# Attention scores of a two-block network: two fp32r passes over stacked exact parts, and the convolution's norm moved from the attention into the gates

## The chip, the cores and the metric

The kernel runs on one core of a Trainium2 chip. The time is the device time of that core in microseconds; before the change three runs gave 3316.32, 3317.76 and 3319.42 us. The core's engines are TensorE (PE, with its weight loads PEld), VectorE (DVE), ScalarE (ACT), GpSimd (POOL) and SyncE (SP, which here issues DMAs). Each engine runs its own instructions in order.

## The reference, cut to what matters

The first block is a mixture of an mLSTM and a spatial gating unit over 512 tokens of width 2048. The second block is two hybrid layers over 528 tokens (16 meta tokens ahead of the 512). In each layer the input is projected to a gated convolution, an attention with 16 heads of 64 on 4 key/value heads, and a recurrence:

```python
c = c_val * sigmoid(c_glu)
c = causal_depthwise_conv(c, conv_dw_w, conv_dw_b)        # 31 taps, 512 channels
c = silu(layer_norm(c, conv_ln_g, conv_ln_b))
c = c @ conv_pw_w + conv_pw_b
y_conv = c * silu(c_gate)
q, k = partial_rotary(q), partial_rotary(k)
# scores q.k / 8 on: the 128 keys before, the query's own block of 128, 16 meta keys
att = sliding_window_sink_attention(q, k, v, sinks)
y_attn = att * silu(a_gate)
y_lru = rg_lru(conv(r_x)) * silu(r_gate)
h = layer_norm(alpha * h + concat(y_conv, y_attn, y_lru) @ w_out)
```

All of it is float32 and is computed to float32's precision.

## The kernel before, in words

**Products.** A large product a.b is done in three passes of TensorE in the fp32r format (`mm3`, lines 131 to 139): both operands are split into an exact high part (`hi`, a cast on ScalarE) and the rest (`lo`, a subtraction), and hi.hi, hi.lo and lo.hi are added in PSUM. Weights come by DMA in chunks of 512 KB (`weights`, lines 109 to 129): SP loads, ScalarE casts (L125), VectorE subtracts (L128); while `share` is set every other subtraction is GpSimd's. Small products (attention scores, transposes) are plain float32 matmuls, which the trace shows as two records each, a weight load and a matmul twice over.

**Memory.** Most tiles live in one pool of `NSLOT` = 62 slots of 128 x 530 floats (`slot`). A slot is free again when the last reader of its tile is done; who needs one waits. Products of the projections go to two PSUM accumulators (`acc`), small ones to four PSUM banks (`bank`).

**Order.** The kernel is written in one program order; a planner gives every engine its fixed order, ahead of the run, from its own estimate of times: of the instructions that are ready, the one that stands first in the program goes first, and a later one fills a gap. So projections that stand behind the attention in the program run on TensorE between the attention's short matmuls.

**First block's end.** `sgu_all` loops over 8 heads; each has three projections through `acc` (`vps`, `ups`, `zps`). The two tiles `yg` of a head are slots that receive gelu of `ups` (L536) and stay until the block's output product. The normed input holds 32 slots until the last `zps`, the results before hold 16 + 2 a head.

**A layer of the second block** (`layer`, from L860): after the raw projections, for each of two groups g of 8 heads: one projection for keys (`keys`), four for queries (`rotary`), then `attend`. Behind the group 0 come the 8 projections of the convolution (`conv31`: 4 tiles, each a chain of 31 VectorE instructions, L1159 and L1162). Behind group 1 come 16 gate projections (`gate`) with the pointwise product of the convolution (`pointwise`) before the last four. The layer ends with the split of y and the output product (`out2`, `out2_last`).

**Scores.** A tile of q holds two heads, 64 partitions each. Group g's keys are two tiles: `k`, and `kx` with its halves exchanged, each with the 16 meta keys behind every block of 128 keys. `attend_block` (L1047 on) takes four pairs of heads; each head is one float32 matmul with 64 rows (L1064: 128 queries stationary, 272 keys moving, 144 in the first block), the two heads of a pair on the two halves of the array's rows, into a bank each. VectorE adds the mask and takes the maximum (L1067), ScalarE the exponentials, GpSimd and ScalarE scale, TensorE transposes (L1092) and multiplies with the values (L1099).

**The convolution's norm.** `conv_norm` (L1174 on) is a generator in three steps: sums over the channels (GpSimd adds, `halves` on TensorE into two banks), the squares' sums, then the normed tiles and their split. Before, `attend` of group 1 runs one step behind each of its first blocks of queries (`next(others, None)`).

Of the kernel before, what the change touches and what calls it, by code (L numbers as in the profile page):

```python
# [19 lines left out]
P = 128  # L20
# [11 lines left out]
NSLOT = 62  # L32
# [25 lines left out]
def log1p_of_unit(nc, out, e, pool, shape, tag):  # L58
    """out = log(1 + e) for e in [0, 1], by 2*atanh(e / (2 + e))."""
# [13 lines left out]
class Net:  # L73
# [30 lines left out]
    def after(self, ins, other):  # L104
        """Order two instructions for the scheduler (slots of one pool are taken in that order)."""
        self.tc.add_manual_dep(ins.ins, other.ins.name, mybir.DependencyInfo(mybir.DependencyClass.NoSync, mybir.DependencyReason.DATA),
                               reason="slots in order")

    def weights(self, view, more=None):
        """One chunk of weights [P, k, cols] (k * cols <= 1024, with the columns of `more`) as its two exact parts."""  # L110
# [20 lines left out]
    def mm3(self, outs, wh, wl, xh, xl, first, last):  # L131
        """Three passes of (wh + wl)^T (xh + xl) into the regions outs = [(psum, slice of x)]."""
# [8 lines left out]
    def stack(self, name, parts, pool=None, rows=None):  # L141
        """Vectors whose lengths are multiples of 128, as columns of 128 entries on partitions."""
# [18 lines left out]
    def bcast_rows(self, cols, n, ps):  # L161
        """[P, n] per-token columns (token = chunk * 128 + partition) to a row [P, n * 128] on all partitions."""
# [6 lines left out]
    def block1(self):  # L169
        nc, a, tc = self.nc, self.a, self.tc  # L170
        with ExitStack() as ctx:
# [4 lines left out]
            self.cst1 = pool("cst1", 1)  # L176
            self.xT = self.dram.tile([KT, P, S], F32, name="xT")
# [18 lines left out]
    def load_x(self):  # L196
        """x * norm_w with features on partitions, split, and the sums of the tokens' squares."""
# [33 lines left out]
    def norm_x(self):  # L231
        """The same, times the tokens' factors, which are returned as a row."""
# [15 lines left out]
    def proj1(self, col):  # L248
        """Columns [col, col + 256) of x @ w_in, features on partitions: [P, 2 x 512]."""
# [11 lines left out]
    def proj1_tok(self, col, more=None):  # L261
        """The same columns, tokens on partitions: [P, 256] of each chunk, and 16 columns `more` behind them."""
# [10 lines left out]
        for k0, k1 in zip(bounds, bounds[1:]):  # L273
            ks = slice(k0, k1)
            wh, wl = self.weights(w[:, ks], g[:, ks] if g is not None else None)
            for k in range(ks.start, ks.stop):
                for c, o in enumerate(outs):
                    xh, xl = self.Xh[k][:, c * P:(c + 1) * P], self.Xl[k][:, c * P:(c + 1) * P]
                    # the first product of a bank clears it
# [7 lines left out]
    def gates1(self, gs):  # L287
        """From input and forget gates of all heads [token, gate] of each chunk, what the chunks need of them."""
# [53 lines left out]
        # state factors on all partitions: [P, head, chunk]  # L342
# [11 lines left out]
        # 0 where key <= query, else a large negative number: [key, query]  # L354
# [5 lines left out]
    def conv_silu(self, ps, ch, scale, rb=None):  # L360
        """Causal convolution over 4 tokens and silu of one tile of channels (times rb first, where it is given)."""
# [18 lines left out]
    def mlstm_all(self):  # L380
        nc = self.nc
        for pair in range(NH // 2):
# [9 lines left out]
            for j in range(2):  # L392
                h = pair * 2 + j
                vps = self.proj1_tok(2048 + h * 256, 8192 if h == 0 else None)
                # values with a column of ones, split
# [101 lines left out]
    def sgu_all(self):  # L497
        nc, a = self.nc, self.a
        mm = nc.tensor.matmul
        for h in range(NH):  # L500
            ws = self.sm1.tile([P, P], F32, tag="ws", name="ws", bufs=1)
            nc.gpsimd.dma_start(ws, a["w_spatial"][h])
            # keep source <= target; halved, the other half of silu
# [30 lines left out]
            for i in range(2):  # L534
                t = self.slot(S, name="yg")
# [20 lines left out]
    def out1(self):  # L556
        """h = x + y @ w_out; the two norms in one; splits the result for the second block."""
# [12 lines left out]
        for at in range(0, KT, CG):  # L570
# [23 lines left out]
            # before the results' slots are taken, which wait for the products  # L594
# [47 lines left out]
    def raw_split(self, i, z, g, b, t0):  # L642
        """z * g of tile i, split, with g and b as two more tokens."""
# [14 lines left out]
    def normal(self, i, g, b):  # L658
        """Tile i of the layer's input, split."""
# [18 lines left out]
    def from_raw(self, t):  # L678
        """The product with the layer's input, from that with raw [P, 528 tokens, g, b]."""
# [11 lines left out]
    def token_sums(self, sums, chunks):  # L691
        """Sums over partitions of each tile of `sums`, divided by the width: [token, sum, chunk]."""
# [23 lines left out]
    def token_bcast(self, out, col, chunks):  # L716
        """Per-token columns to rows on all partitions, in out[:, chunk]."""
# [142 lines left out]
    def layer(self, l, last):  # L860
# [39 lines left out]
        for i in (0, 1, 2, 3):  # L900
            gate(4 + i, 3072 + i * P)
# [503 lines left out]
```

## Time and profile before

| | before |
|---|---|
| runs | 3316.32, 3317.76 (median), 3319.42 us |
| profiled execution, first to last instruction | 3318.8 us |
| PE busy | 3241.4 us (98%) |
| PEld busy | 2819.8 us |
| DVE busy | 1829.6 us (55%) |
| ACT busy | 1099.5 us (33%) |
| POOL busy | 745.6 us (22%) |
| granted TensorE clock, mean | 0.990 |

The profiled execution is one more execution of the same program; its span is 1.0 us above the runs' median. Busy is the union of an engine's instructions. On PE each record lasts from a matmul's start to its modelled end, and the next one starts before that end, so the distance between starts is what a matmul takes up in a stream.

### The profile page before, as it was taken

What the parts mean: (1) busy time and instruction counts of PE and PEld (TensorE: products, weight loads), DVE (VectorE), ACT (ScalarE), POOL (GpSimd) and SP (SyncE); (2) the same over time, 40 slices, a digit from 0 to 9 for tenths busy, and PEclk for the clock granted to TensorE, in tenths of its full rate; (3) what the DMA queues carried; (4) which work ended last, traced back from release to release, by engine and by line L of the source; (5) the groups of instructions that cost most, each with busy time, mean ns of one, the idle gap of its engine ahead of it and who ended that gap; (6) DMA issues with size and microseconds to landing.
All of it is one profiled execution on the core that took longest, in us unless ns stands there. A gap on an engine that the chain in (4) does not pass through costs nothing. (4 is left out here: it accounts for less than half of the span.)

```text
span 3318.8 us, 46937 instructions
## 1 busy us (share of the span) xinstructions
PE 3241.4 (98%) x19245; PEld 2819.8 (85%) x19245; DVE 1829.6 (55%) x2931; ACT 1099.5 (33%) x1775; POOL 745.6 (22%) x756
## 2 busy tenths in 40 slices
PE   8999999999999999999998999999999999999996
PEld 7888888888888888877778988989999888777885
DVE  8744454534433333556659698352545969634545
ACT  5332323323222222434433533342322353234322
POOL 3000000000100000012355523343244542444302
PEclk9999999999999999999998999999999999999998
DMA  5322222322333333333232222222332222322333
GB/s 185 96 89 89 89 85 88 89 89 84 100 91 93 96 92 94 104 106 104 101 98 68 75 71 64 71 64 84 90 90 77 84 66 64 89 77 70 114 121 108
DMA packets 348280, 299.35 MB, mean 90 GB/s; under 512 B 11312, under 2 KB 313296, under 8 KB 348064
## 3 DMA queue, kind: packets, MB, share of 16 engines
q1 hardware_dynamic: 343008, 287.35, 28.3%
q0 software_dynamic: 5056, 9.00, 1.0%
q8 instruction: 151, 2.47, 0.3%
q14 instruction: 65, 0.53, 0.1%
HBM read 287.91 MB, written 8.39 MB: 89 GB/s over the span
## 5 line engine op out<-in xcount | busy, mean ns | idle before, releaser
L125 ACT CAST whi<-raw 128x1024 fp32r<-128x1024 f32 (+1 forms) x526 | 549.6, 1045 | 1461.9 <-PE acc L137 1076.0
L128 DVE TENSOR_TENSOR wlo<-raw,whi 128x1024 fp32r<-128x1024 f32 (+1 forms) x456 | 582.2, 1277 | 798.4 <-ACT whi L125 790.9
L139 PE MATMUL acc<-Xh,wlo 128*128 128x512 f32 x1280 | 509.1, 398 | 0.0
L135 PE MATMUL acc<-Xh,whi 128*128 128x512 f32 x1280 | 507.7, 397 | 1.4 <-ACT Xh L223 1.4
L137 PE MATMUL acc<-Xl,whi 128*128 128x512 f32 x1280 | 504.9, 394 | 1.7 <-DVE Xl L224 1.7
L139 PE MATMUL acc<-Hh,wlo 128*128 128x264 f32 (+1 forms) x1792 | 447.7, 312 | 1.3 <-POOL wlo L128 1.3
L137 PE MATMUL acc<-Hl,whi 128*128 128x264 f32 (+1 forms) x1792 | 445.8, 311 | 0.0
L135 PE MATMUL acc<-Hh,whi 128*128 128x264 f32 (+1 forms) x1792 | 444.7, 311 | 0.3 <-ACT xr L675 0.3
L139 PEld LDWEIGHTS acc<-Hh,wlo 128*128 128x128 f32 x1792 | 292.4, 189 | 29.1 <-issue 10.2
L137 PEld LDWEIGHTS acc<-Hl,whi 128*128 128x128 f32 x1792 | 291.8, 189 | 27.7 <-issue 10.1
L135 PEld LDWEIGHTS acc<-Hh,whi 128*128 128x128 f32 x1792 | 292.0, 189 | 24.2 <-issue 5.8
L139 PEld LDWEIGHTS acc<-Xh,wlo 128*128 128x128 f32 x1280 | 241.1, 188 | 57.0 <-issue 2.2
L137 PEld LDWEIGHTS acc<-Xl,whi 128*128 128x128 f32 x1280 | 241.0, 188 | 56.5 <-DVE Xl L224 2.2
L135 PEld LDWEIGHTS acc<-Xh,whi 128*128 128x128 f32 x1280 | 241.0, 188 | 53.2 <-ACT Xh L223 1.8
L284 PE MATMUL acc<-whi,Xl 128*128 128x256 f32 x960 | 269.5, 281 | 0.0
L282 PE MATMUL acc<-whi,Xh 128*128 128x256 f32 x960 | 269.5, 281 | 0.0
L283 PE MATMUL acc<-wlo,Xh 128*128 128x256 f32 x960 | 269.4, 281 | 0.0
L128 POOL TENSOR_TENSOR wlo<-raw,whi 128x1024 fp32r<-128x1024 f32 x70 | 180.2, 2575 | 326.9 <-ACT whi L125 306.8
L1162 DVE SCALAR_TENSOR_TENSOR conv<-cth,dw,conv 128x527 f32<-128x527 f32 (+18 forms) x240 | 218.2, 921 | 3.0
L282 PEld LDWEIGHTS acc<-whi,Xh 128*128 128x128 f32 x960 | 180.6, 188 | 0.9 <-issue 0.4
L283 PEld LDWEIGHTS acc<-wlo,Xh 128*128 128x128 f32 x960 | 180.4, 188 | 0.4
L284 PEld LDWEIGHTS acc<-whi,Xl 128*128 128x128 f32 x960 | 180.7, 188 | 0.0
(532 smaller groups left out, 5421.7 us busy)
## 6 DMA issues: line engine op xcount, KB each, us to landing
raw<-in_w_in_dram SPq DMA_DIRECT2D x380, 512.0 KB, 3.6
raw<-in_w_out_dram SPq DMA_DIRECT2D x136, 512.0 KB, 3.7
xt<-in_x_dram SPq DMA_DIRECT2D x16, 256.0 KB, 7.7
xT<-xraw POOLq DMA_DIRECT2D x16, 256.0 KB, 4.1
xr<-xT SPq DMA_DIRECT2D x16, 256.0 KB, 4.5
out_dram<-zt SPq DMA_DIRECT2D x16, 256.0 KB, 2.1
raw<-in_conv_pw_w_dram SPq DMA_DIRECT2D x4, 512.0 KB, 3.3
raw<-in_w_in_dram SPq DMA_DIRECT2D x4, 384.0 KB, 3.1
```

Of the source, the lines that this page charges most:

```text
L125: nc.scalar.copy(hi, raw)
L128: eng.tensor_tensor(lo, raw, hi.bitcast(F32), op=SUB)
L135: mm(o, wh, xh[:, s], start=first, stop=False)
L137: mm(o, wh, xl[:, s], start=False, stop=False)
L139: mm(o, wl, xh[:, s], start=False, stop=last)
L282: mm(o, xh, wh[:, k - k0, :], start=first, stop=False, **f)
L283: mm(o, xh, wl[:, k - k0, :], start=False, stop=False, **f)
L284: mm(o, xl, wh[:, k - k0, :], start=False, stop=(k == KT - 1), **f)
L1162: nc.vector.scalar_tensor_tensor(c[:, s:], th[:, :L2 - s], self.pc["dw"][:, j, i:i + 1], c[:, s:], MUL, ADD)
```

## The change

The slots go from 62 to 60, and the key pool `kp` from 2 to 4 tiles. In the first block the last head's two `yg` tiles get a pool of their own. A pair of query heads becomes two tiles, one per head, each with the head's high part on one half of the partitions and its low part on the other half. A key head becomes two tiles, its high part on both halves and its low part on both halves. A head's scores are then two fp32r matmuls over 128 rows: (high, low) of q times the high part of k, and times its low part; all four products are in the sum. `conv_norm` is started behind the attention, and its steps stand behind the first three gates. The end of `split_y` takes four of its 16 low parts from `kp` instead of two. Comments and docstrings are dropped, which changes line numbers only.

```diff
-NSLOT = 62
+NSLOT = 60
+            self.more1 = pool("more1", 2)
-                t = self.slot(S, name="yg")
+                t = self.more1.tile([P, S], F32, tag="yg", name="yg") if h == NH - 1 else self.slot(S, name="yg")
-            self.kp = pool("kp", 2)
+            self.kp = pool("kp", 4)
-            self.attend(g, qs, last, self.conv_norm(cs, parts) if g else iter(()))
+            self.attend(g, qs, last)
...
+        norm = self.conv_norm(cs, parts)
         for i in (0, 1, 2, 3):
             gate(4 + i, 3072 + i * P)
+            next(norm, None)
...
     def rotary(self, ps, t0):
+        nc = self.nc
         t, sh = self.rotated(ps, t0)
-        q = self.slot(name="q")
-        self.nc.gpsimd.tensor_tensor(q[:, t0:], t, sh, op=ADD)
-        return q
+        nc.gpsimd.tensor_tensor(t, t, sh, op=ADD)
+        qs = [self.slot(L2, F32R, "q") for _ in range(2)]
+        lower, upper = slice(0, 64), slice(64, P)
+        for q, a, b in zip(qs, (lower, upper), (upper, lower)):
+            nc.scalar.copy(q[a, t0:], t[a])
+            nc.vector.tensor_tensor(q[b, t0:], t[a], q[a, t0:].bitcast(F32), op=SUB)
+        return qs
...
     def keys(self, ps):
         nc = self.nc
         t, sh = self.rotated(ps, 0)
-        k, x = (self.kp.tile([P, NCH, KB], F32, tag="k", name=n) for n in ("k", "kx"))
+        nc.gpsimd.tensor_tensor(t, t, sh, op=ADD)
...
-        nc.gpsimd.tensor_tensor(k[:, :, :P], blocks(t), blocks(sh), op=ADD)
-        nc.gpsimd.tensor_tensor(k[:, :, P:], meta(t), meta(sh), op=ADD)
-        for i in range(2):
-            nc.scalar.copy(x[64 - 64 * i:128 - 64 * i], k[64 * i:64 * i + 64])
-        self.k = [v.rearrange("p n k -> p (n k)") for v in (k, x)]
+        self.k = []
+        for s in range(2):
+            src = t[64 * s:64 * s + 64]
+            hi, lo = (self.kp.tile([P, NCH, KB], F32R, tag="k", name=n) for n in ("kh", "kl"))
+            for i in range(2):
+                h, l = hi[64 * i:64 * i + 64], lo[64 * i:64 * i + 64]
+                for cs, view in ((slice(0, P), blocks), (slice(P, KB), meta)):
+                    nc.scalar.copy(h[:, :, cs], view(src))
+                    nc.vector.tensor_tensor(l[:, :, cs], view(src), h[:, :, cs].bitcast(F32), op=SUB)
+            self.k.append([v.rearrange("p n k -> p (n k)") for v in (hi, lo)])
+
+    def scores(self, ps, qs, p, i, qc, kc):
+        for j, k in enumerate(self.k[p // 2]):
+            self.nc.tensor.matmul(ps, qs[p][i][:, qc], k[:, kc], start=j == 0, stop=j == 1)
...
-            if n >= 0:
-                next(others, None)
...
-                h = slice(64 * i, 64 * i + 64)
-                mm(pss[i], qs[p][h, qc], self.k[p // 2 ^ i][h, k0:k0 + w], start=True, stop=True)
+                self.scores(pss[i], qs, p, i, qc, slice(k0, k0 + w))
...
-            lo = (self.slot(L2, F32R, "y2l") if k < KT - 3 else
+            lo = (self.slot(L2, F32R, "y2l") if k < KT - 5 else
                   (self.kp if k < KT - 1 else self.sp).tile([P, L2], F32R, tag="k" if k < KT - 1 else "s", name="y2l"))
```

## Rows read from the trace of the kernel before

**Rows 1.** The page's first part: busy us, share of the span, instructions.

```profile
span 3318.8 us, 46937 instructions
PE 3241.4 (98%) x19245; PEld 2819.8 (85%) x19245; DVE 1829.6 (55%) x2931; ACT 1099.5 (33%) x1775; POOL 745.6 (22%) x756
```

**Rows 2.** Windows: length, then busy us of PE, PEld, DVE, ACT, POOL; clock, DMA.

```profile
1920.00:2060.00 140.00, 138.50 (x992) 121.15 (x993) 136.40 (x230) 47.71 (x118) 42.68 (x36) 1.00 0.22 65
2060.00:2100.00 40.00, 38.22 (x302) 35.13 (x302) 11.84 (x19) 6.91 (x9) 16.47 (x11) 1.00 0.24 68
...
2720.00:2860.00 140.00, 140.00 (x924) 119.92 (x923) 133.84 (x204) 44.13 (x98) 41.01 (x31) 1.00 0.21 61
```

**Rows 3.** Windows of the score line L1064 alone: length, busy us of PE, PEld.

```profile
1900.00:2060.00 160.00, 17.21 (x64) 7.58 (x64) 1.00 0.22 65
...
sum 600.00, PE 61.44 PEld 28.59; mean PE 15.36 PEld 7.15
```

**Rows 4.** Timeline of PE, layer 0, group 0: start us, length us, instruction.

```profile
1991.06 0.49 PE L1064 MATMUL sb<-k,q 64*128 64x272 f32 x1
1991.07 0.49 PE L1064 MATMUL sb<-kx,q 64*128 64x272 f32 x1
...
1991.72 0.51 PE L139 MATMUL acc<-Hh,wlo 128*128 128x264 f32 x2
...
1995.10 0.41 PE L135 MATMUL acc<-Hh,whi 128*128 128x264 f32 x2
1995.34 0.40 PE L137 MATMUL acc<-Hl,whi 128*128 128x264 f32 x2
...
1997.05 0.28 PE L139 MATMUL acc<-Hh,wlo 128*128 128x264 f32 x1
1997.26 0.72 PE L1064 MATMUL sb<-k,q 64*128 64x272 f32 x2
1997.91 0.39 PE L139 MATMUL acc<-Hh,wlo 128*128 128x264 f32 x1
1998.14 0.28 PE L135 MATMUL acc<-Hh,whi 128*128 128x264 f32 x1
```

**Rows 5.** The same timeline, scores of the first block of queries.

```profile
1916.47 0.28 PE L1064 MATMUL sb<-k,q 64*128 64x144 f32 x1
...
1916.59 0.28 PE L1064 MATMUL sb<-k,q 64*128 64x144 f32 x1
```

**Rows 6.** Groups by form: count, busy us, mean ns, idle before and its releaser.

```profile
L44 DVE TENSOR_TENSOR Xl<-xs,Xh 128x512 fp32r<-128x512 f32 x16 | 10.7, 680 | 0.0
L43 ACT CAST ch<-conv 128x528 fp32r<-128x528 f32 x8 | 5.0, 628 | 10.6 <-DVE conv L1203 10.6
```

**Rows 7.** Timeline at the last head of `sgu_all`, and one head before it.

```profile
1331.46 1.09 ACT L536 ACTIVATE yg<-acc 128x512 f32<-128x512 f32 x2 [1.68 <-PE acc L137]
...
1236.79 0.28 PE L284 MATMUL acc<-whi,Xl 128*128 128x256 f32 x1
...
1237.10 1.02 ACT L520 ACTIVATE vg<-acc 128x1024 f32<-128x1024 f32 x1 [4.62 <-PE acc L284]
```

**Rows 8.** Groups by form: the two instructions that read `zps` of `sgu_all`.

```profile
L552 DVE SCALAR_TENSOR_TENSOR thz<-thz,acc 128x512 f32<-128x512 f32 x16 | 10.9, 683 | 0.0
L551 ACT ACTIVATE thz<-acc 128x512 f32<-128x512 f32 x16 | 9.5, 596 | 11.2 <-DVE thz L552 11.2
```

**Rows 9.** Timeline of layer 1, group 1: the norm's first step, then the pointwise product.

```profile
2922.54 1.32 POOL L1178 TENSOR_TENSOR csum<-conv 128x528 f32<-128x528 f32 x1
...
2932.38 1.05 PE L1170 MATMUL half<-csum,ones 128*128 128x264 f32 x4
...
2933.36 0.49 PE L1064 MATMUL sb<-k,q 64*128 64x272 f32 x1
...
3031.52 0.39 PE L1064 MATMUL sb<-k,q 64*128 64x272 f32 x1
...
3045.29 0.40 PE L135 MATMUL acc<-ch,whi 128*128 128x512 f32 x1
```

More of the change, by code (lines that the diff above doesn't have):

```diff
@@ L967, in keys, with attend @@
         t, sh = self.rotated(ps, 0)
-        k, x = (self.kp.tile([P, NCH, KB], F32, tag="k", name=n) for n in ("k", "kx"))
+        nc.gpsimd.tensor_tensor(t, t, sh, op=ADD)
         blocks, meta = (lambda v: v[:, META:].rearrange("p (n k) -> p n k", n=NCH),
-                        lambda v: v[:, None, :META].to_broadcast([P, NCH, META]))
-        nc.gpsimd.tensor_tensor(k[:, :, :P], blocks(t), blocks(sh), op=ADD)
-        nc.gpsimd.tensor_tensor(k[:, :, P:], meta(t), meta(sh), op=ADD)
-        for i in range(2):
-            nc.scalar.copy(x[64 - 64 * i:128 - 64 * i], k[64 * i:64 * i + 64])
-        self.k = [v.rearrange("p n k -> p (n k)") for v in (k, x)]
-    def attend(self, g, qs, last, others):
+                        lambda v: v[:, None, :META].to_broadcast([v.shape[0], NCH, META]))
+        self.k = []
[11 more added lines that the diff above has]
+            self.nc.tensor.matmul(ps, qs[p][i][:, qc], k[:, kc], start=j == 0, stop=j == 1)
+    def attend(self, g, qs, last):
         nc = self.nc
@@ L1000, in attend_meta @@
             for i in range(2):
-                h = slice(64 * i, 64 * i + 64)
-                mm(pss[i][:META, p * META:(p + 1) * META], qs[p][h, :META], self.k[p // 2 ^ i][h, P:KB],
-                   start=True, stop=True)
+                self.scores(pss[i][:META, p * META:(p + 1) * META], qs, p, i, slice(0, META), slice(P, KB))
         pm2 = pm.rearrange("q (p i) k -> q p i k", i=2)
@@ L1062, in attend_block @@
             for i in range(2):
-                h = slice(64 * i, 64 * i + 64)
-                mm(pss[i], qs[p][h, qc], self.k[p // 2 ^ i][h, k0:k0 + w], start=True, stop=True)
+                self.scores(pss[i], qs, p, i, qc, slice(k0, k0 + w))
             t = self.sp.tile([P, 2, 2 * P + META], F32, tag="s", name="s")[:, :, :w]
```

## The prediction, made before the changed kernel ran

> **What bounds the kernel now.** I read the page's busy line first: PE is busy 3241.4 of 3318.8 us, DVE 55% [rows 1]. That is an average, so next come the windows around the attention. While group 0's attention runs beside the convolution's chain, PE is busy 138.50 of 140 us in layer 0 and 140.00 of 140 in layer 1, and DVE is nearly as full: 136.40 and 133.84 [rows 2]. So PE sets the pace, with projections that the planner puts between the attention's short matmuls; but there DVE has only 3.6 us and 6.2 us of 140 free. Third, the score line alone: its 256 records (64 in each of four windows) keep PE busy for 61.44 us [rows 3]. Busy ends at a matmul's modelled end, so last comes the timeline, where the distance between starts tells what PE really gives up [rows 4].
>
> **The scores: what goes.** Two projection matmuls start 0.24 us after the two before (1995.10, 1995.34), so one takes 0.12 us. Around a head that runs alone, the projection matmul ahead of it takes 0.21 (1997.05 to 1997.26), the head's two records 0.65 (to 1997.91) and the projection matmul behind it 0.23 (to 1998.14): 1.09 for what would be 0.24 without the head, so a head costs 0.85 us where its busy time is 0.72 [rows 4]. The factor is 1.18, and 61.44 x 1.18 = 72.5 us is what the 128 heads cost PE in both layers [rows 3, 4]. The bounds: 61.4 (busy time alone) and about 100, an estimate with all heads alone (96 wide ones at 0.85, 32 narrow ones at some 0.6); 72.5 lies between because some heads run in pairs.
>
> **The scores: what comes.** 256 fp32r matmuls over all 128 rows: 192 of 272 columns and 64 of 144. A projection is the same kind of matmul at 264 columns and 0.12 us [rows 4]; by columns, 272 take 0.125: 24.1 us. No row shows fp32r at 144 columns. In proportion to the columns it is 0.066 us; a plain float32 record of 144 columns starts 0.12 us after the one before [rows 5], and an fp32r matmul that needed two such records' time would take 0.24. I take 0.12, the nearest row: 7.7 us (4.2 to 15.4). They have the projections' form, so I take nothing for the switch into and out of half rows; at worst 0.09 + 0.11 stay around each of 128 heads, 26 us. Sum 31.8, so 72.5 - 31.8 = 40.7, rounded down to **40.5 us**, go. The ends are -4 (61.4 less 39.5 with the slow narrow ones, less 26) and 72 (100 less 28.3); I keep to the middle, since the busy sum and the factor are measured. The meta tokens' scores have 16 x 16 columns and as many records as before: nothing.
>
> The Trainium skill, "TensorE: Matmul & The Clock Gate", section "Part 3: Packing small matmuls", speaks against this part: contractions under 128 rows placed in different row groups run side by side, and so two heads cost what one costs. The trace shows that it can be so: the heads started at 1991.06 and 1991.07 and the next matmul at 1991.72 [rows 4]. It also shows the head at 1997.26 alone. By the rule the 64 pairs would cost about 0.85 x 48 + 0.6 x 16 = 50 us, and 18 us would go; this is a rival below, worked out there from rows.
>
> **The parts of q and k: what is added.** Each of 16 query tiles gets two casts on ACT and two subtractions on DVE, on 64 partitions; each of 4 key tiles eight and eight (half of them 64 columns long) where there were two copies. At 0.68 us a subtraction and 0.63 a cast [rows 6], DVE gets 16 x 1.36 + 4 x 3.5 = 36 us and ACT some 28. GpSimd's add stays, and the keys' two adds become one. No row shows 64 partitions or an output on other partitions than the input; between nothing and double I take the row's price. On its engine each subtraction stands in line with mask, convolution and weight subtractions, and the scores of the group wait for the last of them, about 3 us later than now. That is hidden: projections of the convolution (group 0) or gates (group 1) stand ready. For group 0 the splits come before the full DVE stretch, for group 1 mostly behind it, where DVE is 11.84 of 40 us busy [rows 2]. The price if that cover fails is the second rival's. I take **+3 us** for PE waits in the full stretches (0 to 20).
>
> **Sixty slots: the first block.** At head 6 the slots hold 32 of input, 16 results, and 14 `yg`: 62. The trace has the proof that this was the brim: at head 7 gelu waited 1.68 us for a projection matmul, until `zps` had released input [rows 7]. With 60 slots head 6 is the one that waits, until `zps` of head 7 (head 7 itself has its own pool). Till then one of the two accumulators is held, so `zps` 6, `vps` 7, `ups` 7 and `zps` 7 share the other, and PE stops three times while it is read out. After `vps`: last matmul 1236.79, read from 1237.10 to 1238.12 [rows 7], PE free since 1236.91: 1.2 us. After `ups`: two gelu, 1.09 us [rows 7], and the same start: 1.4. After `zps`: two tanh of 0.60 and a product of 0.68 behind the second [rows 8], with the start 2.2. Sum **+4.8 us** (0, if the planner finds other slots, to 9, at double). In the second block I count exactly 60 slots in group 1's attention (32 input, 4 values, 4 recurrence, 4 + 4 results, 4 convolution, 8 q), so nothing waits there but the norm.
>
> **The norm moves.** Its step 1 now stands between group 1's blocks: the sums' four matmuls ran at 2932.38 and the next scores only behind them, at 2933.36 [rows 9]. Behind the attention it no longer delays it; I take **-2 us** for waits that go (0 to -5). It can begin when q's slots come free, at the last scores (3031.52 in layer 1), and the pointwise product started 14 us later, at 3045.29 [rows 9]. Its chain alone: 7 GpSimd passes at 1.32, ten Newton instructions and about 14 other full-length ones on DVE at 0.68, partly side by side: some 30 us, an estimate from [rows 6, 9]. So the pointwise product is late by some 16 us. What hides it are the four gates behind it in the program, each 48 matmuls of 512 columns (0.23 us by columns from [rows 4]), 11 us, which need nothing of it; and without the norm inside it the attention ends earlier. I take 0.
>
> **The sum.** 3318.8 - 40.5 + 3 + 4.8 - 2 = 3284.1 for the profiled execution, whose own time is its span. The runs' median of 3317.8 lies 1.0 lower; so **3283 us**.
>
> **The rivals.** *First: DVE keeps the pace in the full stretches.* Group 0's saving, half of 40.5, comes back as waits there: 3283 + 20 = 3303. For it: 97% of DVE in [rows 2]. Against: PE was 99 to 100% busy in the same windows, and behind the first one DVE has room for what is left over.
> *Second, on the other side: the splits stop PE.* If all 36 us of added subtractions land on DVE where it is full, PE waits them out and loses group 0's saving as well: 3303 + 36 = 3339. It decides once the added work in such a stretch is above DVE's free 4 to 6 us; 9 us belong to each group. Against: group 0's share stands ahead of that stretch.
> *Third: the norm is late.* If the planner has used up the four gates before the pointwise product is ready, each layer's end waits the 16 us above, and some 4 more (an estimate) until the late results are through gate and split: 20 us a layer, 3283 + 40 = 3323. Against: four gates hold 44 us.
> *Fourth: most heads already ran side by side*, a pair costing 0.85 as one head does: 18 us go instead of 40.5, so 3283 + 22 = 3305 (64 pairs: 0.85 x 48 + 0.6 x 16 = 50 us, less 31.8). Against: the records of [rows 4] that stand alone, and 61.44 us busy [rows 3] where pairs throughout would show about 42 (48 x 0.73 + 16 x 0.45, estimates from [rows 4, 5]). It is the rule of the Trainium skill named above.
> *Fifth: nothing is won*, because the planner, with other estimates, orders the whole layer anew and loses as much elsewhere: 3318.
>
> **How the numbers follow.** Forecast 0.60, with its own range 3268 to 3297 (the score terms' nearer ends, 144 columns, first block 0 to 9, waits 0 to 10). First rival 0.17, fourth 0.05, third 0.08, second 0.05, fifth 0.05. About 0.2%, 6.6 us, is what a measurement of this kernel tells from no change, so the borders are 3311 and 3324. Faster: 0.60 + 0.17 + 0.05 = 0.82. The fifth and half of the third (on the border) are no change: 0.09. The second and the other half are slower: 0.09. The range 3268 to 3311 takes in the first and the fourth and leaves out somewhat under two in ten.
>
> **What would show it.** The score line's matmuls over 128 rows and 128 x 272 at distances near 0.125 us, without 0.2 us gaps around them; their 144-column records between 0.066 and 0.24 apart. PE gaps of 1 to 2 us at the last two heads of `sgu_all`, and gelu of head 6 behind `zps` 7. Scores of group 1 following each other faster in layer 1 than the 100 us from 2933.36 to 3031.52. PE still above 97% in the full stretches. Wrong would be: PE gaps released by `kl`, `q` or a convolution tap; a pointwise product that PE waits for; or score matmuls that take as long as before.

## The result and the profile after

The change made the kernel slower. Four runs of it gave 3339.22 to 3345.69 us, median 3341.89; four of the kernel before, timed beside it, 3315.69 to 3319.42, median 3317.04. The ratio is 1.0075 (95% interval 1.0061 to 1.0090). The forecast was 3283 us, with a range of 3268 to 3311. The profiled execution of the changed kernel spans 3343.9 us, 25.1 more than before.

The page's first part, as in [rows 1]:

```profile
span 3343.9 us, 47053 instructions
...
PE 3225.7 (96%) x19245; PEld 2831.7 (85%) x19245; DVE 1878.1 (56%) x2995; ACT 1125.9 (34%) x1831; POOL 737.5 (22%) x752
```

TensorE has as many instructions as before and less to do, and the span is longer: the difference is TensorE waiting, and running at its lower clock behind waits. The scores themselves did what the change says. The timeline of PE where heads stand alone among projections, to be read beside [rows 4]:

```profile
1961.11 0.41 PE L135 MATMUL acc<-Hh,whi 128*128 128x264 f32 x2
1961.36 0.29 PE L994 MATMUL sb<-kh,q 128*128 128x272 f32 x1
1961.49 0.29 PE L994 MATMUL sb<-kl,q 128*128 128x272 f32 x1
1961.61 0.41 PE L137 MATMUL acc<-Hl,whi 128*128 128x264 f32 x2
...
1990.37 1.08 PE L1112 MATMUL att<-pt,vt 128*64 128x256 f32 x4 [0.72 <-DVE pt L1108]
1991.37 0.40 PE L994 MATMUL sb<-kh,q 128*128 128x272 f32 x1
1991.61 0.29 PE L994 MATMUL sb<-kl,q 128*128 128x272 f32 x1
```

Starts lie 0.12 to 0.13 us apart, and the projections on both sides lose nothing. Behind products that use half of the array's columns (`128*64`, 1990.37) the first score takes 0.24 (1991.37 to 1991.61). The 144-column ones start 0.113 us apart in the median. Over all heads, distance to the next start with what the neighbours lose, the scores cost 73.0 us before and 40.6 after: 32.4 us went.

Where the rest of TensorE's time is, by part of the kernel. A part runs from its first matmul to the next part's first; a wait is idle time over 0.1 us between two matmuls; low clock is what distances between starts are longer while the clock is at half; the last column is the remainder of the difference, the scores above all.

| part | before | after | difference | waits | low clock | remainder |
|---|---|---|---|---|---|---|
| first block's projections | 1346.1 | 1356.3 | +10.2 | +6.8 | +2.7 | +0.7 |
| its output and the raw projections | 461.3 | 461.4 | +0.1 | +0.6 | -0.5 | 0.0 |
| layer 0 | 525.0 | 525.6 | +0.6 | +9.5 | +7.3 | -16.2 |
| output and raw projections | 277.3 | 276.0 | -1.3 | -0.3 | -1.6 | +0.6 |
| layer 1 | 490.0 | 505.7 | +15.7 | +24.4 | +5.0 | -13.7 |

So the scores' 30 us are in both layers, and they are given back as waits and low clock, with more on top. What PE waited for (us in all, times, longest), first in the first block's last heads, where before the longest wait of this stretch was below 0.3:

```profile
PE acc L283 <- DVE thz L553: 4.1, 1, 4.1
PE acc L135 <- ACT vg L521: 1.1, 1, 1.1
PE acc L135 <- ACT yg L537: 0.8, 1, 0.8
```

Then in layer 1, where before all waits but 0.5 us were two of 1.9 on `pm`:

```profile
PE acc L135 <- ACT ch L43: 15.5, 1, 15.5
PE ptm L1053 <- POOL pm L1091: 4.5, 1, 4.5
PE half L1183 <- POOL csq L1204: 2.6, 1, 2.6
PE att L1112 <- DVE pt L1108: 2.0, 2, 1.4
PE att L1058 <- DVE ptm L1055: 2.0, 3, 1.1
```

Two kinds stand there. The first and the third line are the pointwise product (`ch`) and the norm's second sums (`csq`), the others are the attention's own chain: its transposes wait for the softmax (`pm` is its result for the meta keys, which is transposed first), and its products for copies out of the banks. Layer 0 shows the second kind:

```profile
PE att L1112 <- DVE pt L1108: 3.4, 2, 2.7
PE att L1058 <- DVE ptm L1055: 3.2, 2, 3.0
PE ptm L1053 <- POOL pm L1091: 2.8, 2, 1.9
```

The windows of group 0's full stretches, which answer to [rows 2] some 10 to 15 us later, show the same: PE has gone from 138.50 and 140.00 to about 136, while DVE is as full as it was.

```profile
1930.00:2070.00 140.00, 135.68 (x1043) 127.27 (x1042) 135.85 (x231) 50.05 (x123) 44.37 (x32) 0.99 0.22 65
...
2735.00:2875.00 140.00, 136.39 (x938) 121.46 (x937) 136.57 (x208) 48.31 (x107) 43.82 (x31) 1.00 0.24 69
```

The norm in layer 1, which answers to [rows 9]: the channels are added up by 2937.7 (a POOL row), the last scores run at 3014.25, and only behind the attention's last transposes do the sums reach TensorE (PE rows).

```profile
2936.38 1.32 POOL L1193 TENSOR_TENSOR csum<-csum,conv 128x528 f32<-128x528 f32 x1
```

```profile
3014.25 0.29 PE L994 MATMUL sb<-kl,q 128*128 128x272 f32 x1
...
3039.64 0.61 PE L1183 MATMUL half<-csum,ones 128*128 128x264 f32 x2
...
3054.72 1.58 PE L1183 MATMUL half<-csq,ones 128*128 128x264 f32 x4 [2.63 <-POOL csq L1204]
...
3071.76 1.22 PE L135 MATMUL acc<-ch,whi 128*128 128x512 f32 x2 [15.46 <-ACT ch L43]
```

From the sums to the pointwise product are 32.1 us. The twelve gates ahead of it in the program were used up at 3052; the four behind it began at 3098.

### The profile page after: what moved, and what is told of

It reads as the page before. It is cut to its first block, busy times and chain, and to the rows that moved or that the text cites. A ratio compares the mean times of both kernels' runs of the same rounds, so it can differ in the third digit from the quotient of the medians.

```text
span 3343.9 us, 47053 instructions
## 1 busy us (share of the span) xinstructions
PE 3225.7 (96%) x19245; PEld 2831.7 (85%) x19245; DVE 1878.1 (56%) x2995; ACT 1125.9 (34%) x1831; POOL 737.5 (22%) x752
## 5 line engine op out<-in xcount | busy, mean ns | idle before, releaser
L135 PE MATMUL acc<-Xh,whi 128*128 128x512 f32 x1280 | 507.8, 397 | 3.7 <-ACT Xh L224 1.8
L137 PE MATMUL acc<-Xl,whi 128*128 128x512 f32 x1280 | 505.7, 395 | 1.2 <-DVE Xl L225 1.2
L135 PE MATMUL acc<-Hh,whi 128*128 128x264 f32 (+1 forms) x1792 | 444.6, 311 | 1.1 <-ACT cth L1169 0.8
L135 PEld LDWEIGHTS acc<-Hh,whi 128*128 128x128 f32 x1792 | 293.2, 189 | 18.5 <-ACT cth L1169 0.9
L135 PEld LDWEIGHTS acc<-Xh,whi 128*128 128x128 f32 x1280 | 241.1, 188 | 56.5 <-ACT Xh L224 2.2
L1175 DVE SCALAR_TENSOR_TENSOR conv<-cth,dw,conv 128x515 f32<-128x515 f32 (+25 forms) x240 | 220.3, 936 | 2.6
```

The costliest lines, as they stand in the source:

```text
L135: mm(o, wh, xh[:, s], start=first, stop=False)
L137: mm(o, wh, xl[:, s], start=False, stop=False)
L1175: nc.vector.scalar_tensor_tensor(c[:, s:], th[:, :L2 - s], self.pc["dw"][:, j, i:i + 1], c[:, s:], MUL, ADD)
```

## The experiments

Four theories. A: the norm is late, because its sums wait for the attention's banks and the four last gates can't fill TensorE ahead of the pointwise product. B: the attention's copies stand in VectorE's full queue. C: the added subtractions fill VectorE. D: the missing slots stop the first block. Each run that follows was timed beside the kernel before on the same chip (medians 3318.3 to 3319.7 us). The planner orders each edited program anew, so an edit can also move instructions that it doesn't name.

**e1: the norm's two sums go to one of the two accumulators each (`halves_acc`), not to banks.**

```diff
-        m = self.halves(self.ones, s)
+        m = self.halves_acc(self.ones, s)
...
-        for ps, hs in self.halves(self.ones, q):
+        for ps, hs in self.halves_acc(self.ones, q):
```

> The changed kernel, but the two pairs of channel sums of the convolution's norm go to one of the two accumulators instead of two of the four small PSUM banks; nothing else. Theory A (the norm's sums queue for a bank behind all banks of the attention, so that the pointwise product is late and TensorE stands 18 us in layer 1 and then runs some 20 us at the lower clock): the sums follow their adds at once, TensorE no longer waits for the pointwise product, and the time falls by some 25 to 35 us, to 3307 to 3317 us. Rival B (the norm waits for slots of the shrunken pool): the sums stay at the attention's end, 3342. Rival C (the loss is the added subtractions on VectorE): 3342 as well, with the gap before the pointwise product gone and others in its place.

Measured: 3386.42 us, ratio 1.0202 (1.0188 to 1.0216), 44.5 us above the changed kernel. The time went the other way than expected, and that teaches something. The sums did run early (2948.82 in layer 1), so they had waited for banks. But now projections stop. The windows of line L135 alone (length, PE, PEld, clock) in layer 0, between the sums at 2121.8 and the squares' sums at 2186.2, and a wait over the whole kernel:

```profile
2130.00:2140.00 10.00, 3.89 (x18) 2.85 (x18) 1.00 0.19 54
2140.00:2186.00 46.00, 0.00 (x0) 0.00 (x0) 0.78 0.04 12
```

```profile
PE ptm L1053 <- POOL pm L1091: 37.0, 7, 8.2
```

For 46 us no projection runs, and the attention's waits, which projections had filled, lie open. That fits accumulators taken in the program's order (no run shows it apart from the rest): the gates stand behind the squares' sums, so none can have an accumulator before these have had theirs.

**e2: the norm's steps back between group 1's blocks.**

```diff
-            self.attend(g, qs, last)
+            self.attend(g, qs, last, self.conv_norm(cs, parts) if g else iter(()))
...
-        norm = self.conv_norm(cs, parts)
...
-            next(norm, None)
...
+            if n >= 0:
+                next(others, None)
```

> The changed kernel with the norm's steps put back between the blocks of group 1's attention, as before (its three squares' tiles come from the small work pool instead of slots); scores, parts of q and k and 60 slots stay. Theory A: the pointwise product is on time again and the time falls by 25 to 35 us, to 3307 to 3317 us; the attention of group 1 takes longer than in the changed kernel. Rival C (VectorE's added subtractions are what costs): it stays within 5 us of 3342.

Measured: 3333.26 us, 1.0047 (1.0035 to 1.0060), 8.6 below the changed kernel, between the two sides of the expectation. Layer 1 is 12.5 us shorter and has no wait at the pointwise product. Layer 0, which had lost little to the norm, is 6.0 longer, with a new wait of 7.1 us on `pm` at 2135. So A holds for layer 1, and it is not all.

**e3: the pool of two extra tiles at head 6, not head 7.**

```diff
-                t = self.more1.tile([P, S], F32, tag="yg", name="yg") if h == NH - 1 else self.slot(S, name="yg")
+                t = self.more1.tile([P, S], F32, tag="yg", name="yg") if h == NH - 2 else self.slot(S, name="yg")
```

> The changed kernel, but the two extra tiles of the first block go to head 6 of the gating unit and not to head 7. Theory D (with 60 slots head 6 holds an accumulator until head 7's last projection, TensorE stands three times and falls to the lower clock): the first block ends 10 us earlier, the three gaps at 1288 to 1340 us are gone, 3332 us. Rival: the delay comes from another place of the first block, 3342.

Measured: 3331.91 us, 1.0040 (1.0028 to 1.0053): 10.0 us go, and the three waits of the first block with them (1345.5 us, 1356.3 in the changed kernel). D is settled.

**e4: the kernel before with the norm alone moved.**

```diff
-            self.attend(g, qs, last, self.conv_norm(cs, parts) if g else iter(()))
+            self.attend(g, qs, last, iter(()))
...
+        norm = self.conv_norm(cs, parts)
         for i in (0, 1, 2, 3):
             gate(4 + i, 3072 + i * P)
+            next(norm, None)
```

> The kernel before with one part of the change alone: the norm is started behind the attention and its steps stand behind the first three gates; scores, slots and pools as before. Theory A: the sums queue for banks behind the attention, the pointwise product is late in both layers and the time rises by 25 to 35 us, to 3342 to 3352 us, more than the whole change does. Rival B (slots): with 62 slots and four fewer tiles of q nothing waits, 3317. Rival C: 3317.

Measured: 3337.21 us, 1.0055 (1.0043 to 1.0068), 18.9 us above before, 5 less than theory A's lower end. Layer 0 takes what it took, layer 1 takes 20.4 us more, and the wait is the changed kernel's:

```profile
3061.62 1.22 PE L135 MATMUL acc<-ch,whi 128*128 128x512 f32 x2 [17.16 <-ACT ch L43]
```

This part is the move's own price, whatever the scores cost.

**f1: e2 and e3 together.** Only the scores and the splitting are left of the change.

> The changed kernel with the norm's steps back between group 1's blocks and the extra pool given to head 6: what is left of the change is the scores and the splitting of queries and keys. If the two measured parts add up (norm back -8.6 us, head 6 -10.0 us against 3341.9): 3323 us, so 32 us less of TensorE time in the scores bring nothing, and group 0's stretches keep their 17 us of TensorE gaps in the two layers. Rival (the scores' gain reaches the end once the other two parts are gone): 3285 to 3300 us.

Measured: 3328.04 us, 1.0029 (1.0019 to 1.0039), 9.7 us above before. That is 5 us above the sum of the two parts, and what is left, with 32 us less of scores, is still slower than before. Waits on `pm` are 14.9 us in six places.

**f2: e3, with low parts written by ScalarE as plain copies; the subtraction is left out.**

```diff
-            nc.vector.tensor_tensor(q[b, t0:], t[a], q[a, t0:].bitcast(F32), op=SUB)
+            nc.scalar.copy(q[b, t0:], t[a])
...
-                    nc.vector.tensor_tensor(l[:, :, cs], view(src), h[:, :, cs].bitcast(F32), op=SUB)
+                    nc.scalar.copy(l[:, :, cs], view(src))
```

> The changed kernel with the extra pool at head 6, and with the 64 low parts of queries and keys written by ScalarE as plain copies (the subtraction is left out, so the low parts' values are not computed): VectorE loses the 42 us that the change added. Theory C (the added subtractions fill VectorE in group 0's stretches): the gaps of group 0 fall from 17 to about 5 us in the two layers and the low clock behind them goes, 3332 - 18 = 3314 us. Rival (VectorE sets the pace there with the work it had before, since TensorE has become faster): gaps stay above 12 us, 3326 to 3333 us.

Measured: 3335.79 us, 1.0052 (1.0039 to 1.0065), 3.9 above e3 and above both sides of the expectation. VectorE loses 40 us (1837.9 busy), ScalarE gets 31.6 (1158.0 busy), and nothing is won: C gets no support, though ScalarE's added copies may have cost something as well. Most of these subtractions don't stand where VectorE is full: group 0 of layer 0 has 150.1 us of VectorE in 163.1, where the changed kernel has 157.3 in 169.5.

**f3: e3, with the four last gates' projections ahead of the pointwise product.** `gate_factor` is `gate` without its last product.

```diff
+        ths = [self.gate_factor(self.inproj2(l, 1024 + i * P, t0), t0) for i in range(4)]
         self.pointwise(l, *parts, last)
         for i in range(4):
-            gate(i, 1024 + i * P)
+            nc.gpsimd.tensor_tensor(self.y[i][:, t0:], self.y[i][:, t0:], ths[i], op=MUL)
```

> The changed kernel with the extra pool at head 6, and the four last gates' projections (with tanh and product on VectorE) written ahead of the pointwise product, only their last product behind it. Theory A (the norm is late, and the four last gates stand behind the pointwise product in TensorE's order, so they can't hide it): layer 1's gap of 15 to 18 us and the low clock behind it (10 us) go, 3332 - 22 = 3310 us (3306 to 3316). Rival (the chain of norm, pointwise product, gate and split at the layer's end is the bound, wherever gates stand): within 5 us of 3332.

Measured: 3318.07 us, 0.9998 (0.9988 to 1.0007), 13.8 below e3. The pointwise product starts at 3083.57 without a wait. The gain is less than the 22 expected, since the layer's output product now waits 4.55 and 1.05 us for the split of the pointwise results, which the gates behind had hidden. A holds: the four gates hide the norm if they stand ahead of the pointwise product.

**f4: f3, with the attention's copies out of the banks on ScalarE.**

```diff
-        nc.vector.tensor_copy(ptm[:, :nq], tp[:, :nq])
+        nc.scalar.copy(ptm[:, :nq], tp[:, :nq])
...
-                (nc.vector.tensor_copy if i else nc.scalar.copy)(pt[:, :2 * nh * P], tp[:, :2 * nh * P])
+                nc.scalar.copy(pt[:, :2 * nh * P], tp[:, :2 * nh * P])
```

> As f3, and the attention's copies out of the transposes' banks all on ScalarE (before every other one, and the meta tokens' one, on VectorE). Theory B (group 0's gaps are transposes and products that wait for a copy in VectorE's full queue): gaps in group 0's stretches fall from 17 to under 8 us, 8 to 12 us below f3, about 3300 us. Rival (the wait moves to ScalarE's queue of exponentials and weight casts): within 4 us of f3.

Measured: 3298.52 us, 0.9941 (0.9929 to 0.9954), 19.6 below f3, twice what B expected. The gain is there, but the waits of group 0 did not fall: 8.4 and 7.2 us in the two layers before this edit, 9.0 and 6.7 with it. So B's reason is not the reason; g1 shows which one is.

**g1: the kernel before with f4's copies.**

> The kernel before, with the attention's copies out of the transposes' banks all on ScalarE, as in f4. Theory B (the copies' place in VectorE's queue costs TensorE only since the change, because the shorter scores bring the transposes' turn earlier, while before the change TensorE was the one that others waited for): 3312 to 3320 us, a gain of at most 5 where f4 gained 19.6 over f3. Rival (VectorE's queue delays the attention in the kernel before as well, and the copies are worth the same there whatever the scores cost): 3296 to 3302 us.

Measured: 3295.21 us, 0.9930 (0.9918 to 0.9943). The rival holds: the copies are worth 23.3 us in the kernel before as well, and have nothing to do with the change. The timeline shows where the time goes. In the kernel before, four products of the values take 1.08 us, once per half of the columns:

```profile
1980.31 1.08 PE L1099 MATMUL att<-pt,vt 128*64 128x256 f32 x4
...
1983.29 1.08 PE L1099 MATMUL att<-pt,vt 128*64 128x256 f32 x4 [0.58 <-DVE pt L1095]
```

With both copies on ScalarE, one behind the other (ACT, then PE, of g1), eight take 1.09:

```profile
1972.39 1.07 ACT L1095 COPY pt<-ptb 128x512 f32<-128x512 f32 x2 [3.21 <-PE ptb L1092]
```

```profile
1975.36 1.09 PE L1099 MATMUL att<-pt,vt 128*64 128x256 f32 x8
```

The two halves of the columns run side by side here, where both operands came from one engine, one behind the other. Of the 224 products of the values, 94 start within 0.025 us of the next, where 30 did, and all of them take 33.9 us instead of 50.0 (distances between starts). These 16 us, with 4 of the scores, reach the end: the two layers are 20.9 us shorter, and PE waits there as long as before (12.4 us for 13.4). f4 does the same in the changed kernel: 78 pairs for 31, 38.2 us for 51.2; most of the rest of its 19.6 us is shorter waits and less low clock in the two layers (2.7 and 3.8 us).

**g2 and h3: f4 with two, and with three, of the last gates ahead and the rest behind.** The diff is g2's; h3 has 3 and (3,) in place of 2 and (2, 3).

```diff
-        ths = [self.gate_factor(self.inproj2(l, 1024 + i * P, t0), t0) for i in range(4)]
+        ths = [self.gate_factor(self.inproj2(l, 1024 + i * P, t0), t0) for i in range(2)]
         self.pointwise(l, *parts, last)
-        for i in range(4):
+        for i in range(2):
             nc.gpsimd.tensor_tensor(self.y[i][:, t0:], self.y[i][:, t0:], ths[i], op=MUL)
+        for i in (2, 3):
+            gate(i, 1024 + i * P)
```

> As f4, with two of the four last gates ahead of the pointwise product and two behind it. In f4 the output product of layer 1 waited 4.54 and 0.88 us for the split of the last pointwise results, with a stretch of low clock behind, which before had the four gates in front of it. Theory A' (two gates hide the split, two more the norm): 4 to 7 us below f4, 3292 to 3295. Rival (two gates are too few ahead of the pointwise product and TensorE waits for the norm again): 3299 to 3306 us.

> g2 with three of the last four gates ahead of the pointwise product and one behind. g2's gap of 2.44 us ahead of the pointwise product and the low clock behind it (6.8 us long) should go, while one gate still hides the split of the pointwise results: 3290 to 3294 us. Rival (one gate is too few behind it, as none was in f4): 3295 to 3299 us.

Measured: g2 3295.72 us (0.9928, 0.9915 to 0.9940), h3 3284.80 (0.9897, 0.9880 to 0.9913). g2 is 2.8 us below f4, 0.7 above the first side of its expectation; h3 is 5.2 below the first side of its own. The 10.9 us between the two are more than the wait of 2.44 us with its low clock; their profiled executions differ by 6.0, and where the rest comes from was not looked for. h3 is the fastest version that computes all: 33.8 us below before and 10.4 below g1, which has the copies but not the change.

**g3: g2 with two of three weight subtractions on GpSimd.**

```diff
-        self.turn = (self.turn + 1) % 2
+        self.turn = (self.turn + 1) % (3 if self.wmore is not None else 2)
```

> As g2, with two of three weight subtractions on GpSimd while the layers share them, instead of every other one. If VectorE still sets the pace in group 0's stretches (150 of 153 us busy in layer 0): 4 to 10 us below g2, since some 6 us of subtractions leave VectorE in each. Rival (GpSimd's 2.4 us subtractions make weights late, and VectorE's own instructions take twice as long beside GpSimd's, 1.43 us instead of 0.75): 0 to 10 us above g2.

Measured: 3320.75 us, 1.0008 (0.9999 to 1.0017), 25.0 above g2 and outside both expectations. VectorE has 6.3 us less in all (1853.2 busy) and GpSimd 60.4 more (801.1), and waits on `pm` are longer (17.3 us in all, up to 7.7; 12.0 and 5.7 in g2), and weights that GpSimd splits are late for 3.5 us (1.5 in g2). GpSimd also computes `pm`, so a longer queue there can delay the transposes; how much of the 25 us that is was not tried.

**g4 and i2: one of the two passes left out,** in e3 and in h3.

```diff
-        for j, k in enumerate(self.k[p // 2]):
-            self.nc.tensor.matmul(ps, qs[p][i][:, qc], k[:, kc], start=j == 0, stop=j == 1)
+        k = self.k[p // 2][0]
+        self.nc.tensor.matmul(ps, qs[p][i][:, qc], k[:, kc], start=True, stop=True)
```

> The changed kernel with the extra pool at head 6 (3331.9 us), and only the first of the two passes of the scores: the products with the keys' low part are left out. TensorE has 256 matmuls less, 16.0 us by their distances. If TensorE's time in group 0's stretches is worth nothing (VectorE and the planner's order set the pace there): only group 1's half shows, 8 us, 3324. Rival (each us of scores is a us of the kernel): 3316 us.

> h3 with only the first of the two passes of the scores; the products with the keys' low part are left out, 16.0 us of TensorE. If TensorE is again what the layers wait for outside group 0: 6 to 10 us below h3, about 3277 us. Rival (as in g4, TensorE's time in the attention counts for nothing): 3282 to 3288 us.

Measured: g4 3332.83 us (1.0042, 1.0029 to 1.0054), 0.9 above e3; i2 3291.27 (0.9915, 0.9900 to 0.9930), 6.5 above h3, with intervals that still touch, and above both sides of its expectation. Sixteen microseconds less of scores bring nothing in either; for g4 both sides had expected a gain. In g4 the waits of the two layers grow by 9.4 us and the low clock's cost by 3. What e3 waited 7.4 us for, g4 waits 13.6 and 4.7 for, and in layer 1 the earlier gates leave a longer wait for the norm (9.2, from 2.6). The waits view of g4:

```profile
PE acc L135 <- ACT ch L43: 15.1, 2, 14.5
PE ptm L1053 <- POOL pm L1091: 13.6, 4, 5.5
...
PE half L1183 <- POOL csq L1204: 9.2, 1, 9.2
...
PE ptm L1053 <- POOL pm L1030: 4.7, 1, 4.7
```

**h1, h2 and i1: 15 of the convolution's 31 taps left out** in g1, g2 and h3.

```diff
-        for j in range(29, -1, -1):
+        for j in range(29, 14, -1):
```

> g1 with 15 of the convolution's 31 taps left out (120 VectorE instructions, about 90 us over both layers, most of them in group 0's stretches). Before the change TensorE is what others wait for, so little goes: 3283 to 3295 us by either theory. It is the measure for h2.

> g2 with the same 15 taps left out. If VectorE's full queue in group 0's stretches is what eats the scores' gain: h2 falls 10 to 25 us below h1, since nothing else stands between the shorter scores and the end. Rival (the gaps are waits that the planner's order wrote in, ahead of the first block's transposes above all, and their low clock; VectorE's load does not matter): h2 within 5 us of h1.

> h3 with 15 of the 31 taps left out. If the norm's gap and VectorE's load are the two things that ate the scores' gain: h2's 3280.4 less the 10.9 us that the third gate gave, 3270 us (3266 to 3274), 18 us below h1, with the rest of the 32 us in the first block of queries of layer 1 (4.5 us of gap and low clock). Rival (the two overlap): 3276 to 3280.

Measured: h1 3287.71 us (0.9906, 0.9891 to 0.9921), h2 3280.35 (0.9884, 0.9869 to 0.9899), i1 3273.61 (0.9863, 0.9847 to 0.9880). Group 0 of layer 0 in h1, then in h2 (windows; the third busy number is DVE's):

```profile
1911.40:2043.50 132.10, 132.10 (x1016) 119.72 (x1016) 88.18 (x178) 53.41 (x134) 43.40 (x38) 1.00 0.23 67
```

```profile
1911.10:2043.50 132.40, 129.65 (x1029) 122.58 (x1029) 99.47 (x190) 57.49 (x143) 46.24 (x37) 1.00 0.25 73
```

With VectorE 25 to 33% free, the changed kernel is 7.4 us (h2) and 14.1 us (i1) faster than h1, where with all taps it was 0.5 slower (g2) and 10.4 faster (h3). So VectorE's full queue ate 4 to 8 us of the scores' gain, and h2 lies between the two sides of its expectation, i1 at the upper end of its first. What i1 could gain on h1 is less than 32 us: beside the copies on ScalarE the scores of the kernel before cost less (a reckoning like that of the 73.0 and 40.6 us gives 64.0 in h1 and 38.5 in i1), and i1's products of the values take 39.0 us where h1's take 33.9. Of the 20 us that are left, 5.5 are longer waits in the two layers (12.7 for 7.2), and some 14 arrive. In layer 1 of h2 and of i1 the wait at the first block of queries is 4.5 us, as it is with all taps.

## Why the prediction was wrong, step by step

**What bounds the kernel.** "So PE sets the pace" was read off 98 to 100% busy in [rows 2], and with it each microsecond that the scores give back was counted as one of the kernel. This is the step that failed most. f1 has the shorter scores and is slower than the kernel before: in its two layers PE waits 39.4 us for 13.4 before, and low clock costs 11 us more. It isn't that TensorE's time is worth nothing there, since what the values' products saved did arrive, in g1 and in f4. What the step left out is the order. TensorE's is fixed ahead of the run, and with other scores the planner makes another one. At the first block of queries of layer 1 the chain from the first score to the transpose of `pm` took 23.3 us before (2685.6 to 2708.9) and 21.3 after (2700.6 to 2722.0). Before, projections and scores filled all but 1.95 of it. Afterwards the scores in it are shorter and fewer projections stand between them: 121 matmuls, where there were 152. The windows of the tile `acc`, before, then after (length, PE, PEld; the count behind PEld is that of the projections):

```profile
2685.60:2708.90 23.30, 19.62 (x153) 18.69 (x152) 0.00 (x0) 0.00 (x0) 1.00 0.24 69
```

```profile
2700.60:2722.00 21.40, 16.45 (x122) 15.21 (x121) 0.00 (x0) 0.00 (x0) 0.97 0.25 72
```

This is what PE's timeline after shows at its end:

```profile
2717.03 0.40 PE L139 MATMUL acc<-Hh,wlo 128*128 128x264 f32 x2
2721.96 0.47 PE L1053 MATMUL ptm<-ident,pm 128*128 128x128 f32 x1 [4.53 <-POOL pm L1091]
```

The stretch is 2.0 us shorter and the wait for the softmax 2.6 longer; the projections that are gone from it run elsewhere. f1's longest wait on `pm`, 7.05 us at the first block of group 1 in layer 0, is a plainer case: 24 projections stand in that stretch (2112.8 to 2124.8), where the kernel before had 111 (2112.5 to 2128.3) and no wait. So the fifth rival's reason, that the planner orders the layer anew, (given 0.05) is at work beside the softmax's chain. How much of the 32 us each of the two takes, and why the planner puts no further projection there, stays open; no run kept the order or changed the planner's estimates.

**The scores.** The mechanism was right. What went was 32.4 us, not 40.7: the cost before was met (73.0 for 72.5), the cost after mis-sized (40.6 for 31.8), since stretches of low clock and starts behind half-column products were left out. The rule of the Trainium skill that was a rival ("TensorE: Matmul & The Clock Gate", section "Part 3: Packing small matmuls": small matmuls on different parts of the array run at the same time) did not decide the price, though it was at work: of the 256 records of the scores before, half start within 0.025 us of another one, and the other half stood alone, which gives the 73.0 us. g1's eight products in the time of four show it at work on halves of the columns.

**The parts of q and k.** VectorE got 48.5 us in the page, 42.4 of them the subtractions, for 36 forecast. That this stops PE was the second rival, and f2, which took them off VectorE, gained nothing.

**Waits in the full stretches.** Forecast +3. The attention's own lines waited 4.4 us longer in each layer, and some 7.5 us of the added low clock stand behind these waits: 16 us, near the first rival's price of 20 (half of the scores' gain). Its reason, VectorE's pace, accounts for 4 to 8 us by h1, h2 and i1. The rest goes with the order above, and low clock behind its waits; that division is an estimate.

**Sixty slots.** The place was right, at the last two heads, for the reason given (e3). The price was 10.2 us (4.8 forecast, 9 the upper end): the longest stop is 4.12 us where 1.2 to 2.2 were added up, and 2.7 us of low clock behind the stops were not thought of.

**The norm moves.** Two sentences failed. "It can begin when q's slots come free, at the last scores": it began 25.4 us later, behind the last transposes, because its sums take their turn at the banks (with accumulators in place of banks, in e1, they ran early). "What hides it are the four gates behind it in the program": they stand behind the pointwise product, began at 3098 and hid nothing, and ahead of it they did hide it (f3). That the order of the accumulators keeps them behind it fits e1 and is not shown by itself. The chain itself was right (32 us for 30). The third rival had this at 20 us a layer; it came in layer 1 alone, 18.9 us by e4.

**The chances.** The rivals were priced one at a time, as if one of them at most came true. The first and the third came together, with the first block at twice its price: 3283 + 20 + 19 + 5 + 8 (the scores' shortfall) = 3335. The sum is a reckoning afterwards: f1 is 5 us above the sum of its parts, so they don't simply add. Most of what is left is 4.4 us of waits at layer 0's pointwise product and the low clock behind them.

## What to carry to other kernels

An engine that is 98% busy is the bound only as long as its work stays what it is: before a saving there is counted, find the chain that runs beside it in the same stretch, how much of that chain the saved work was filling, and what else will be put in its place: count the projections between the two ends of a chain before and after. A run that leaves out half of the work that remains (g4) costs little and shows whether a further saving would count, with the reserve that it is ordered anew too. When a step is moved, ask which buffers it takes in turn (banks, accumulators) and who stands before it and behind it in that order, not only when its operands are ready.

## What the runs showed of the hardware

**Low clock behind a wait.** The granted clock falls to 0.5, its lower level, inside a wait of 4 us and stays there past its end. Windows of layer 1, around the 15.46 us wait (the third number from the end is the clock):

```profile
3056.00:3072.00 16.00, 0.54 (x2) 0.24 (x2) 13.60 (x16) 1.57 (x3) 7.89 (x6) 0.50 0.11 33
3072.00:3076.00 4.00, 4.00 (x10) 2.93 (x11) 2.86 (x5) 1.79 (x4) 0.00 (x0) 0.52 0.00 0
3076.00:3080.00 4.00, 3.90 (x15) 2.19 (x13) 2.04 (x3) 1.53 (x4) 0.00 (x0) 1.00 0.02 4
```

The long wait costs 2 us more behind it, the 4.53 us wait at 2722 about 2.8 (half clock from 2720.8 to 2727.6): a short wait is dear by its own measure. The two waits on `pm` in layer 1 of the kernel before, 1.95 and 1.92 us long, had none behind them.

**VectorE beside GpSimd.** While GpSimd adds (POOL row), a VectorE instruction with two inputs takes 1.68 us that takes 0.71 alone:

```profile
2696.92 1.48 POOL L965 TENSOR_TENSOR rt<-rt,rs 128x512 f32<-128x512 f32 x1
2697.28 1.68 DVE L1153 SCALAR_TENSOR_TENSOR lr<-lr,lt 128x528 f32<-128x528 f32 x1
...
2709.61 0.71 DVE L1153 SCALAR_TENSOR_TENSOR lr<-lr,lt 128x528 f32<-128x528 f32 x1
```

Of the convolution's 240 taps, the 66 that overlap a GpSimd instruction take 1.43 us in the mean and the others 0.75. The Trainium skill's "SBUF — State Buffer", section "Who interferes with whom", says that the two engines share a pair of ports under an exclusive lock, and that a VectorE instruction with two inputs from SBUF contends with a GpSimd instruction that reads SBUF; these rows agree.
